# The seventh weight block of a seven-product set: summed ahead into a buffer of its own, or made in place by a difference at its own step

## The chip, the core and the metric

The kernel runs on one core of a Trainium2 chip. The metric is the time of one execution in device microseconds (us); a time quoted for a kernel is the median of several executions. One of the executions was recorded by the hardware profiler, and every row of a profile in this document comes from such a recording.

The engines go by the names of the profile: PE (TensorE) multiplies matrices, and PEld is its loading of weights; DVE (VectorE), ACT (ScalarE) and POOL (GpSimd) work on elements; SP issues transfers. POOL and SP each feed DMA queues of their own.

## What is computed

One block of a language model over 512 tokens of 1024 features, in float32:

```python
x = x + 0.5 * swiglu(rmsnorm(x, g1), w_gu1, w_down1)
x = x + hybrid_mixer(rmsnorm(x, gm), ...)
x = x + 0.5 * swiglu(rmsnorm(x, g2), w_gu2, w_down2)
return rmsnorm(x, final_g)

def swiglu(x, w_gu, w_down):             # 1024 -> 2 x 2816 -> 1024
    g, u = jnp.split(x @ w_gu, 2, axis=-1)
    return (jax.nn.silu(g) * u) @ w_down

def hybrid_mixer(h, ...):
    cb, cc, cu, q, k, v, g_lr, r, ga, gb = split(h @ w_in)
    y_conv = (cb * causal_short_conv(cc * cu, conv_w)) @ w_out_conv
    o = gla_chunked(q, k, v, log_a)      # gated linear attention, 64-token chunks, 4 heads
    y_gla = (rmsnorm_per_head(o) * silu(r)) @ w_out_gla
    return (sigmoid(ga) * y_conv + sigmoid(gb) * y_gla) @ w_o
```

## The kernel before

**Products.** Nearly all of the work is products with weights. Each weight block of 512 KB (128 partitions by 1024 numbers) is loaded into a tile `f`, and is split into two parts that TensorE multiplies faster: ACT casts it to a high part `wh` (line 409), and DVE subtracts that from the block to get the low part `wl` (line 411). PE multiplies `wh` with the high and the low part of the activations, and then `wl` with the high part. A step of the plan is one weight block with its matmuls: in the rows of the profile 16 matmuls of `wh` and 8 of `wl` (line 575), or 8 of `wh` and 8 of `wl` in a wider form (line 587).

**Sets of seven.** The large products are made in sets. A set covers a 2 x 2 grid of weight blocks a11, a12, a21, a22 and does seven products instead of eight, on sums of blocks. Its steps are called m1, p2, q6, p5, q7, p4 and p3. They need as weights, in this order: a11; a12; then a11+a21+a22 (q6); a21+a22 (p5); **a11+a21 (q7)**; a22 (p4); and for p3 the sum of all that is in a12 by then. A set is named below by the number of its first block in the plan: sets 9 to 41 are the up product of the first FFN, 77 and 81 the values of the attention, 85 to 129 the other columns of `w_in` in the mixer, 141 to 153 its output products, 165 to 197 the up product of the second FFN. The steps of neighbouring sets are interleaved: for a set s and its successor t the order is

```python
seq += [(s, "q6"), (s, "p5"), (s, "q7")]
...
    seq += [(t, "m1"), (s, "p4")]
    seq += [(t, "p2"), (s, "p3")] if i + 2 < n else [(s, "p3")]
```

**The sums of blocks.** Three are made in place by DMAs that add (POOL issues them at line 377, and they show as `f<-f`): a21 += a22 three steps ahead of the set's m1; a11 += a21 right behind the cast and the subtraction of m1; a12 += a11 right behind those of p2. The last one *reads* a11; it is called the add of p2 below. The weights of q7 are the one sum that is made by DVE (line 389): s3 = a11 + a21 at the same place as the first add and ahead of it in the program, since it needs a21 as it was loaded. s3 has a tile of its own. The twelve sets of the two down products ("lean" ones) do it otherwise: they subtract a22 from a11 in place at q7 (line 404).

**Buffers.** There are 10 tiles for raw blocks (`SLOTS`). `slot` gives a new block the tile whose last use, by the plan's step numbers, is earliest. So a set takes five of the ten: four that SP loads (line 350) and s3. `wh` and `wl` have three buffers each.

**What sets the order.** `Weights.take` issues casts and subtractions two steps ahead of the products (`Weights(2)`). The order of the instructions on each engine is then set by a scheduler, from the order in which the program was written and its own estimates; each engine runs its instructions in that order and waits at each until what it needs is there. On DVE, between the subtractions of line 411, stand the other uses of the results: line 657 is the sum that takes a product's value out of its PSUM bank (`quarter`), lines 635 and 642 are sums of two halves of a wide bank (`bb`), and lines 561, 1611 and 1625 are elementwise products and sums of the mixer. In the mixer, p5 of a set uses the PSUM bank that p2 of the same set had, so p5's first matmul needs that set's line 657 to be done. On ACT, lines 633 and 634 copy a wide bank, and line 1590 applies an activation.

Of the kernel before, what the change touches and what calls it, by code (L numbers as in the profile page):

```python
# [56 lines left out]
def unit_cols(u):  # L57
    return u[2] * len(u[3]) * u[4]
# [72 lines left out]
def pieces(half):  # L131
    return [min(2, half - k) for k in range(0, half, 2)]
# [16 lines left out]
def lean(n):  # L149
    return PLAN[n][0].endswith("down")  # L150
# [39 lines left out]
def block_kernel(ctx: ExitStack, tc: tile.TileContext, xT, vecs, gf, gup, wgl, wts, out):  # L190
# [19 lines left out]
    def tile_of(pool, shape, dtype=F32):  # L210
        cnt[0] += 1
        return pools[pool].tile(shape, dtype, tag=pool, name=f"{pool}{cnt[0]}")
# [82 lines left out]
    class Weights:  # L295
# [63 lines left out]
        def load_set(self, n):  # L359

            a = {p: STEPS.index((n, p)) for p in SEQ}
            for i in range(self.issued, a["m1"]):
                if STEPS[i][1] is None and STEPS[i][0] not in self.raw:
                    self.raw[STEPS[i][0]] = self.dma(STEPS[i][0], i)
            a21 = self.dma(n + 2, max(a["p5"], a["m1"] + 3))
            a11 = self.dma(n, a["q7"] if lean(n) else a["p2"] + 3)
            if lean(n):
                self.raw[n] = [a11, None, a21, None, a11]
                return
            a22 = self.dma(n + 3, a["p4"])  # L370
            s3 = self.slot(a["q7"])
            a12 = self.dma(n + 1, a["p3"])
            self.raw[n] = [a11, a12, a21, a22, s3]

# [5 lines left out]
        def issue(self):  # L380
            at = self.issued
            self.fetch(at)
            for n in self.loads.get(at, ()):
                self.load_set(n)
            for n in self.sums.get(at, ()):
                a11, a12, a21, a22, s3 = self.raw[n]
                w = unit_cols(PLAN[n])
                if not lean(n):
                    nc.vector.tensor_tensor(out=s3, in0=a11, in1=a21, op=ALU.add)
                self.first[n] = (self.add(a21[:, :w], self.block(n + 3), self.added) if lean(n)  # L390
                                 else self.add(a21, a22))
            for n, i in self.more.get(at, ()):
                a = STEPS.index((n, ("p3", "p4")[i // 2]))
                self.raw[n][i] = self.dma(n + i, a)
            n, p = STEPS[at]
            w = unit_cols(PLAN[n])
            if p is None:
                raw = self.raw[n]
            else:
                a11, a12, a21, a22, s3 = self.raw[n]  # L400
                raw = {"m1": a11, "p2": a12, "q6": a11, "p5": a21, "q7": s3, "p4": a22,
                       "p3": a12}[p]
            if p == "q7" and lean(n):
                nc.vector.tensor_tensor(out=a11[:, :w], in0=a11[:, :w], in1=a22[:, :w],
                                        op=ALU.subtract)
            late = at >= len(STEPS) - len(pieces(HALVES[-1]))
            h = tile_of("op" if late else "wh", [P, 1024], F32R)
            l = tile_of("op" if late else "wl", [P, 1024], F32R)
            self.cast = nc.scalar.copy(h[:, :w], raw[:, :w]).ins  # L409
            with ExitStack() if self.lead is None else tc.issue_after(self.lead):  # L410
                nc.vector.tensor_tensor(out=l[:, :w], in0=raw[:, :w],  # L411
                                        in1=h[:, :w].bitcast(F32), op=ALU.subtract)
            self.lead = None
            if p == "m1":
                twin = n + 4 if STEPS[at + 1] == (n + 4, "m1") else n
                self.add(a11[:, :w], a21[:, :w], self.first[twin])
            if p == "p2":
                self.add(a12[:, :w], a11[:, :w])
            self.issued += 1
            self.ready.append((h, l))  # L420
# [1446 lines left out]
```

## Time and profile before

| | us |
|---|---|
| median of 3 runs | 1142.9 (1142.2 to 1143.33) |
| the profiled execution | 1147.98 |
| its span in the trace | 1146.3 |
| PE busy | 1134.4 (99%) |
| DVE busy | 1001.4 (87%) |
| ACT busy | 713.2 (62%) |
| POOL busy | 135.4 (12%) |
| mean granted clock of PE | 0.998 |

The profiled execution is 1.7 us longer than its span, and 5.1 us longer than the median of the others. A row of the timeline gives the start in us from the start of the span, the duration in us, the engine, the line, the operation, what it writes and reads, how many instructions were drawn together (x8), and in square brackets how long the engine had been idle before it and what ended that. A row of groups gives the same without a start, with the total busy time and the mean in ns, and behind it the idle time before these instructions. A row of waits gives who waited, for whom, the total in us, how many times, and the longest.

### The profile page before, as it was taken

To read this page: it belongs to the slowest core of one execution; us is meant where nothing else is said; L and a number is where in the kernel's file an instruction comes from. 1 tells how busy PE (TensorE), PEld (TensorE's weight loads), DVE (VectorE), ACT (ScalarE), POOL (GpSimd) and SP (SyncE) were. 2 spreads that over 40 slices of the span, in tenths; PEclk is the share of its full clock that TensorE was granted. 3 is DMA by queue.
4 is the path that set the end of the run, shared out by engine and by line. 5 is a ranking of instruction groups with operands and counts; after the bars stand their busy time and mean duration, and the time that the engine had idled before them with its cause. 6 is when DMAs were issued, how large, how long until landed. Compare 5 with 4: busy or idle time off the path is not lost.

```text
span 1146.3 us, 17367 instructions
## 1 busy us (share of the span) xinstructions
PE 1134.4 (99%) x6574; PEld 1002.6 (87%) x6574; DVE 1001.4 (87%) x1247; ACT 713.2 (62%) x967; POOL 135.4 (12%) x178
## 2 busy tenths in 40 slices
PE   9999999999999999999999999999999999999997
PEld 7888888988888889999999988999888888898886
DVE  7998888889888977979799889699899888889987
ACT  8576666667455656666666567555747665666645
POOL 1111111111110111100101100110001101112100
PEclk9999999999999999999999999999999999999999
DMA  9477777869574588876869756577537888977941
GB/s 348 100 195 187 200 176 192 193 146 289 141 258 130 118 195 237 201 188 171 231 159 245 184 162 208 132 172 189 151 92 202 199 228 220 226 184 181 267 105 73
DMA packets 74403, 214.28 MB, mean 187 GB/s; under 512 B 8176, under 2 KB 20592, under 8 KB 74320
## 3 DMA queue, kind: packets, MB, share of 16 engines
q0 software_dynamic: 21376, 76.03, 35.8%
q1 hardware_dynamic: 48304, 132.67, 34.7%
q10 hardware_dynamic: 4640, 4.49, 1.2%
q8 instruction: 51, 0.84, 0.3%
q14 instruction: 32, 0.26, 0.1%
HBM read 133.46 MB, written 11.53 MB: 126 GB/s over the span
## 4 chain that ended last, share of the span: by engine, by line
PE 98%; ACT 1%; DMA 0%; DVE 0%; issue 0%; SPq 0%; ACTq 0%
PE mm L892 16%; PE mm L575 15%; PE bb L587 12%; PE mm L468 9%; PE w L587 9%; PE z L587 8%; PE y L587 7%; PE aux L892 6%; PE mm L482 5%; PE x L587 4%; PE y L575 2%; PE z L575 1%; PE aux L575 1%; PE aux L1501 1%; PE x L575 1%; DMA f<-wts 0%
## 5 line engine op out<-in xcount | busy, mean ns | idle before, releaser
L409 ACT CAST wh<-f 128x1024 fp32r<-128x1024 f32 (+1 forms) x366 | 375.1, 1033 | 284.9 <-PE mm L575 40.7
L411 DVE TENSOR_TENSOR wl<-f,wh 128x1024 fp32r<-128x1024 f32 (+1 forms) x366 | 434.4, 1196 | 52.3 <-ACT wh L409 50.3
L377 POOL DMA_DIRECT2D f<-f x132 | 114.0, 866 | 896.6 <-DVE wl L411 591.0
L892 PE MATMUL mm<-wh,op 128*128 128x512 f32 x536 | 133.7, 389 | 0.0
L575 PE MATMUL mm<-op,wh 128*128 128x256 f32 x960 | 125.7, 284 | 0.0
L575 PEld LDWEIGHTS mm<-op,wh 128*128 128x128 f32 x960 | 119.8, 192 | 0.4
L892 PEld LDWEIGHTS mm<-wh,op 128*128 128x128 f32 x536 | 100.4, 188 | 20.7
L587 PE MATMUL bb<-op,wh 128*128 128x512 f32 x384 | 98.7, 399 | 2.6 <-ACT tp L634 2.3
L587 PEld LDWEIGHTS bb<-op,wh 128*128 128x128 f32 x384 | 69.9, 191 | 15.8 <-ACT tp L634 2.5
L468 PE MATMUL mm<-op,wh 128*128 128x512 f32 x320 | 75.8, 389 | 0.0
L892 PE MATMUL mm<-wl,op 128*128 128x512 f32 x268 | 72.8, 389 | 0.0
L587 PE MATMUL w<-op,wh 128*128 128x512 f32 x288 | 71.8, 391 | 0.1
L468 PEld LDWEIGHTS mm<-op,wh 128*128 128x128 f32 x320 | 60.0, 188 | 12.5
L575 PE MATMUL mm<-op,wl 128*128 128x256 f32 x480 | 67.5, 283 | 0.0
L587 PE MATMUL z<-op,wh 128*128 128x512 f32 x256 | 63.8, 391 | 0.0
L575 PEld LDWEIGHTS mm<-op,wl 128*128 128x128 f32 x480 | 61.9, 192 | 0.1
L587 PEld LDWEIGHTS w<-op,wh 128*128 128x128 f32 x288 | 52.7, 188 | 10.3 <-ACT tp L765 0.3
L892 PEld LDWEIGHTS mm<-wl,op 128*128 128x128 f32 x268 | 50.3, 188 | 10.4
L587 PEld LDWEIGHTS bb<-op,wl 128*128 128x128 f32 x384 | 52.8, 192 | 3.9
L587 PE MATMUL y<-op,wh 128*128 128x512 f32 x224 | 55.9, 391 | 0.0
L587 PEld LDWEIGHTS z<-op,wh 128*128 128x128 f32 x256 | 46.8, 188 | 8.9
L587 PE MATMUL bb<-op,wl 128*128 128x256 f32 x384 | 53.8, 283 | 0.0
(321 smaller groups left out, 1914.4 us busy)
## 6 DMA issues: line engine op xcount, KB each, us to landing
f<-wts SPq DMA_DIRECT2D x215, 512.0 KB, 4.6
f<-f POOLq DMA_DIRECT2D x128, 512.0 KB, 5.2
f<-wts POOLq DMA_DIRECT2D x10, 512.0 KB, 8.8
turn<-tp SPq DMA_DIRECT2D x12, 256.0 KB, 3.6
f<-wts SPq DMA_DIRECT2D x10, 256.0 KB, 4.6
X<-xT SPq DMA_DIRECT2D x8, 256.0 KB, 6.1
xs<-X POOLq DMA_DIRECT2D x8, 256.0 KB, 5.2
tp<-ga SPq DMA_DIRECT2D x8, 256.0 KB, 5.5
```

The costliest lines, as they stand in the source:

```text
L377: self.added = nc.gpsimd.dma_start(out_, a, accum_op=ALU.add).ins
L409: self.cast = nc.scalar.copy(h[:, :w], raw[:, :w]).ins
L411: nc.vector.tensor_tensor(out=l[:, :w], in0=raw[:, :w], in1=h[:, :w].bitcast(F32), op=ALU.subtract)
L468: nc.tensor.matmul(o, w[:, i * P : (i + 1) * P], a[k], start=j == k == 0, stop=j == 2 and k == kt - 1)
L482: nc.tensor.matmul(o[c], w[:, s : s + P], a[k], start=k == 0 and j == 0, stop=k == kt - 1 and j == 2)
L575: nc.tensor.matmul(o[:, e * HW : (e + 1) * HW], w[:, k * HW + e * P : k * HW + (e + 1) * P], a(k), start=self.fresh and j == k == e == 0, ...
L587: nc.tensor.matmul(o[:, e, :n], w[:, k * HW + e * P : k * HW + (e + 1) * P], a(k), start=self.fresh and i == k == 0, stop=i == 1 and k == ...
L892: nc.tensor.matmul(o[t], a(k)[:, t * P : (t + 1) * P], ww[:, i * 512 : (i + 1) * 512], start=fresh and j == k == 0, stop=j == 2 and k == s ...
L1501: nc.tensor.matmul(o[:, b], v[t][:, vc : vc + P], sc[:, b], start=True, stop=t == 0)
```

## The change

For every set whose q7 stands more than two steps behind its p2, the sum s3 and its tile are dropped. a11's tile is kept until q7, and at q7's own step DVE subtracts a22 from it in place, as the lean sets do: a11 is by then a11+a21+a22, so the result is a11+a21. Six sets keep the sum (41, 77, 81, 129, 145 and 197); the 12 lean ones stay as they were; 30 change: eight in each FFN, eleven in the mixer (85 to 125) and 141, 149 and 153.

```diff
             a21 = self.dma(n + 2, max(a["p5"], a["m1"] + 3))
-            a11 = self.dma(n, a["q7"] if lean(n) else a["p2"] + 3)
+            same = lean(n) or a["q7"] - a["p2"] > 2
+            a11 = self.dma(n, a["q7"] if same else max(a["q7"], a["p2"] + 3))
             if lean(n):
                 self.raw[n] = [a11, None, a21, None, a11]
                 return
             a22 = self.dma(n + 3, a["p4"])
-            s3 = self.slot(a["q7"])
+            s3 = a11 if same else self.slot(a["q7"])
             a12 = self.dma(n + 1, a["p3"])
             self.raw[n] = [a11, a12, a21, a22, s3]
@@ in issue(), three steps ahead of m1
-                if not lean(n):
+                if s3 is not a11:
                     nc.vector.tensor_tensor(out=s3, in0=a11, in1=a21, op=ALU.add)
@@ in issue(), at the step itself
-            if p == "q7" and lean(n):
+            if p == "q7" and s3 is a11:
                 nc.vector.tensor_tensor(out=a11[:, :w], in0=a11[:, :w], in1=a22[:, :w],
                                         op=ALU.subtract)
```

In the changed kernel the lines behind the first edit stand one further down: the sum is line 390, the subtraction in place 405, the cast 410, the low part 412, and lines 561, 635, 642, 657, 1611 and 1625 are 562, 636, 643, 658, 1612 and 1626.

Two places in the order of DVE show what moves. The rows are those of the program, each with its line, operation, output, inputs and shape; the number behind a tile's name only tells tiles apart. The first is set 113, in the mixer, from q6 to q7. Before, where `f_5294` is this set's s3, `f_5290` its a11, `f_5288` its a21, and the row at the top makes s3 of the next set, 117:

```order
L389 TENSOR_TENSOR f_5537<-f_5533,f_5531 128x1024
L1611 SCALAR_TENSOR_TENSOR y_3208<-tp_5618,tp_5345 128x2x256
L411 TENSOR_TENSOR wl_5626<-f_5290,wh_5625 128x1024
L657 TENSOR_TENSOR tp_5595<-mm_5622,tp_5595 128x512
L411 TENSOR_TENSOR wl_5655<-f_5288,wh_5654 128x1024
L657 TENSOR_TENSOR tp_5480<-mm_5493,tp_5480 128x512
L561 TENSOR_TENSOR qk_3210<-g_598_3489,qk_3210 128x512
L561 TENSOR_TENSOR y_3208<-acc_5560,tp_5480 128x2x256
L561 TENSOR_TENSOR g_598_3489<-g_597_3488,qk_3210 128x256
L561 TENSOR_TENSOR g_598_3489<-qk_3210,sm 128x256
L561 TENSOR_TENSOR g_597_3488<-g_597_3488,qk_3210 128x4x64
L411 TENSOR_TENSOR wl_5689<-f_5294,wh_5688 128x1024
```

The same stretch of DVE after, from p5 on, where `f_5274` is a11 and `f_5276` a22:

```order
L412 TENSOR_TENSOR wl_5636<-f_5272,wh_5635 128x1024
L658 TENSOR_TENSOR tp_5463<-mm_5476,tp_5463 128x512
L562 TENSOR_TENSOR qk_3202<-g_590_3481,qk_3202 128x512
L562 TENSOR_TENSOR y_3200<-acc_5542,tp_5463 128x2x256
L562 TENSOR_TENSOR g_590_3481<-g_589_3480,qk_3202 128x256
L562 TENSOR_TENSOR g_590_3481<-qk_3202,sm 128x256
L562 TENSOR_TENSOR g_589_3480<-g_589_3480,qk_3202 128x4x64
L405 TENSOR_TENSOR f_5274<-f_5274,f_5276 128x1024
L636 TENSOR_TENSOR tp_5690<-tp_5690,tp_5691 128x512
L562 TENSOR_TENSOR qk_3202<-g_588_3479,qk_3202 128x512
L562 TENSOR_TENSOR g_589_3480<-g_590_3481,sm 128x4x64
L412 TENSOR_TENSOR wl_5671<-f_5274,wh_5670 128x1024
```

The sum of the next set is gone from its place ahead of q6, and this set's subtraction stands behind the three `g` products, with three small instructions between it and the low part of q7.

The second place is set 121, from q6 to q7. Before, `f_5758` is a11 and `f_5762` s3, and `tp_6073<-mm_6100` takes p2's value out of the bank that p5 needs:

```order
L642 TENSOR_TENSOR tp_6073<-bb_6051,tp_6073 128x512
L642 TENSOR_TENSOR tp_6096<-bb_5806,tp_6096 128x512
L411 TENSOR_TENSOR wl_6104<-f_5758,wh_6103 128x1024
L1625 SCALAR_TENSOR_TENSOR y_3208<-tp_6096,y_3208 128x2x256
L657 TENSOR_TENSOR tp_6073<-mm_6100,tp_6073 128x512
L411 TENSOR_TENSOR wl_6134<-f_5756,wh_6133 128x1024
L1625 SCALAR_TENSOR_TENSOR y_3208<-tp_6073,y_3208 128x2x256
L553 RECIPROCAL st_so<-st_so 128x64
L657 TENSOR_TENSOR tp_5967<-mm_5972,tp_5967 128x512
L411 TENSOR_TENSOR wl_6164<-f_5762,wh_6163 128x1024
```

After, with `f_5740` for a11 and `f_5742` for a22:

```order
L643 TENSOR_TENSOR tp_6053<-bb_6031,tp_6053 128x512
L412 TENSOR_TENSOR wl_6083<-f_5740,wh_6082 128x1024
L643 TENSOR_TENSOR tp_6076<-bb_5787,tp_6076 128x512
L405 TENSOR_TENSOR f_5740<-f_5740,f_5742 128x1024
L1626 SCALAR_TENSOR_TENSOR y_3200<-tp_6076,y_3200 128x2x256
L658 TENSOR_TENSOR tp_6053<-mm_6080,tp_6053 128x512
L412 TENSOR_TENSOR wl_6113<-f_5738,wh_6112 128x1024
L1626 SCALAR_TENSOR_TENSOR y_3200<-tp_6053,y_3200 128x2x256
L658 TENSOR_TENSOR tp_5948<-mm_5953,tp_5948 128x512
L412 TENSOR_TENSOR wl_6144<-f_5740,wh_6143 128x1024
```

The subtraction stands right behind q6, so ahead of the row of line 658 that frees p5's bank and ahead of p5's low part. Set 125 has the same order. The order of PE's products, the banks and the buffers of `wh` and `wl` are the same in both kernels.

## The prediction, on record before the changed kernel ran

> **What bounds the kernel.** I read the page first: busy time, and the chain that ended last.
>
> ```profile
> PE 1134.4 (99%) x6574; PEld 1002.6 (87%) x6574; DVE 1001.4 (87%) x1247; ACT 713.2 (62%) x967; POOL 135.4 (12%) x178
> PE 98%; ACT 1%; DMA 0%; DVE 0%; issue 0%; SPq 0%; ACTq 0%
> ```
>
> PE is busy for 1134.4 of 1146.3 us, and 98% of the chain runs over it. A change of the weights' making can therefore hardly help; it can only hurt, by making PE wait. What it could win at most is what PE waits now, so the waits of PE came next, the last two once each and short, then the matmuls at the one place that counts, and eight like them from before it:
>
> ```profile
> PE bb L587 <- ACT tp L634: 2.3, 1, 2.3
> ...
> PE mm L482 <- ACT wh L409: 0.7, 1, 0.7
> PE bb L587 <- DVE tp L642: 0.3, 1, 0.3
> 659.06 2.00 PE L587 MATMUL bb<-op,wh 128*128 128x512 f32 x8
> 676.21 3.40 PE L587 MATMUL bb<-op,wh 128*128 128x512 f32 x8 [2.25 <-ACT tp L634]
> 679.41 1.43 PE L587 MATMUL bb<-op,wl 128*128 128x256 f32 x8
> ```
>
> One stall of 2.25 us, and behind it the same eight matmuls take 3.40 instead of 2.00 us. So a stall of that length costs again in speed: 1.40 here, and 1.43 against 1.12 for the eight that follow (1.12 is the usual time, in a row below), 1.7 in all. The windows say where there is little room, each row with the busy time of PE, PEld, DVE, ACT and POOL, the granted clock, the DMA share and GB/s:
>
> ```profile
> 52.00:227.00 175.00, 175.00 (x1060) 156.87 (x1060) 152.03 (x174) 113.30 (x153) 23.39 (x27) 1.00 0.78 189
> 560.00:660.00 100.00, 100.00 (x699) 93.27 (x698) 92.44 (x127) 63.55 (x86) 11.23 (x13) 1.00 0.76 197
> 660.00:690.00 30.00, 27.41 (x177) 24.98 (x176) 24.87 (x30) 20.80 (x29) 0.86 (x1) 0.94 0.60 163
> ```
>
> In the first FFN (52 to 227 us) PE never idles and DVE has 13% left (152.03 of 175). In the mixer (560 to 660) PE still never idles, but DVE has only 7.6 of 100 us left. The stall shows in the third row, at a clock of 0.94.
>
> **The change: what it removes and adds.** Groups by line and form, and waits:
>
> ```profile
> L389 DVE TENSOR_TENSOR f<-f,f 128x1024 f32<-128x1024 f32 x36 | 44.0, 1221 | 4.1 <-DMA f<-wts 3.5
> L404 DVE TENSOR_TENSOR f<-f,f 128x1024 f32<-128x1024 f32 x10 | 12.2, 1223 | 5.7 <-DMA f<-f 5.7
> L411 DVE TENSOR_TENSOR wl<-f,wh 128x1024 fp32r<-128x1024 f32 x350 | 423.9, 1220 | 51.1 <-ACT wh L409 49.1 <-PE mm L1166 0.9 <-issue 0.3
> POOL f L377 <- DVE f L389: 112.5, 25, 24.2
> ACT wh L409 <- DVE f L404: 25.0, 11, 3.5
> DVE f L404 <- DMA f<-f: 6.0, 7, 1.6
> ```
>
> *DVE's work.* 30 sums of 1.221 us go and 30 differences of 1.223 us come: +0.06 us over the kernel, nothing. What changes is when.
>
> *Loads and the first add.* A set takes four tiles of ten instead of five, so SP's loads can start earlier; and a21 += a22 no longer stands behind the sum (POOL waited 112.5 us for it, 25 times). POOL is 12% busy and none of PE's waits above is for a transfer, so I cost both at nothing; the loads' lead hides them before as after. On POOL's and SP's queues nothing new is issued.
>
> *The new wait.* The difference overwrites a11, so it must wait until the add of p2 (a12 += a11) has landed; DVE stands at it meanwhile, with everything that is behind it in its order. And ACT's cast for q7 now waits for the difference: before, s3 lay ready long ahead. The rows of line 404 show both waits in the lean sets: DVE stood 6.0 us in seven cases, ACT 25.0 in eleven, and PE nothing. So the price is set by the cover at each place, which I went through set by set: landing of the add of p2, plus 1.22 for the difference, plus 1.05 for the cast, against the start of q7's matmuls; and what stands behind the difference on DVE, against the matmul that needs it.
>
> *FFN sets (16).* Set 13, from the add of p2 through q6's low part and q7's cast to q7's matmuls, and the transfer times of that stretch:
>
> ```profile
> 67.93 0.86 POOL L377 DMA_DIRECT2D f<-f  x1 [4.70 <-DVE tp L766]
> 73.07 1.23 DVE L411 TENSOR_TENSOR wl<-f,wh 128x1024 fp32r<-128x1024 f32 x1
> 75.06 1.05 ACT L409 CAST wh<-f 128x1024 fp32r<-128x1024 f32 x1 [1.20 <-PE y L587]
> 81.40 0.86 PE L587 MATMUL z<-op,wh 128*128 128x512 f32 x3
> f<-f POOLq DMA_DIRECT2D x24, 512.0 KB, 5.0
> ```
>
> The add is issued at 67.93 and by the median of 5.0 lands at 72.9, before DVE is done with q6 (74.30). The difference then runs to 75.5, the cast to 76.6, and PE wants it at 81.40: 4.8 us of cover, with DVE pushed back by 1.2 in a stretch where it has 13% to spare. The others look like it: 0. If a landing ran some 5 us late here, PE would begin to wait.
>
> *Place A, set 113 (mixer, 590 us).* Here DVE is the cover that fails.
>
> ```profile
> 582.77 1.22 DVE L389 TENSOR_TENSOR f<-f,f 128x1024 f32<-128x1024 f32 x1
> 586.24 1.22 DVE L411 TENSOR_TENSOR wl<-f,wh 128x1024 fp32r<-128x1024 f32 x1
> 589.85 0.42 DVE L561 TENSOR_TENSOR g<-g,qk 128x256 f32<-128x256 f32 x1
> 590.18 1.22 DVE L411 TENSOR_TENSOR wl<-f,wh 128x1024 fp32r<-128x1024 f32 x1
> 590.18 2.00 PE L587 MATMUL bb<-op,wh 128*128 128x512 f32 x8
> 592.02 1.12 PE L587 MATMUL bb<-op,wl 128*128 128x256 f32 x8
> ```
>
> Before, q7's low part (590.18 to 591.40) follows the third `g` product, 0.6 us ahead of its matmul at 592.02, and the high part was cast long ago. After, the difference stands behind that `g` product, and the cast behind the difference. The sum of 1.22 ahead (582.77) is gone, and DVE comes earlier by up to that; I take 1.1, since a sum of line 657 between them can't come before its matmuls end: difference 589.1 to 590.3, cast to 591.35, matmul at 591.4 instead of 590.18. The low part follows behind three small products, at 591.8 to 593.0, and is wanted at 591.4 + 1.84 = 593.2, in time. **+1.2.** Lower end 0 (DVE gains more from the sums that are gone earlier), upper end 2.3 (it gains nothing, and the difference starts when the `g` product ended, 590.27).
>
> *Places B and C, sets 121 and 125.* Here the landing decides. Adds issued over 560 to 690 us, then that of B alone, and the least, middle and longest landing of the two issued at C:
>
> ```profile
> f<-f POOLq DMA_DIRECT2D x14, 512.0 KB, 6.6
> f<-f POOLq DMA_DIRECT2D x1, 512.0 KB, 8.3
> DMA to landing us min/median/max: 4.7/6.5/8.4
> 625.40 0.86 POOL L377 DMA_DIRECT2D f<-f  x1 [3.35 <-DMA f<-f]
> 627.06 1.22 DVE L411 TENSOR_TENSOR wl<-f,wh 128x1024 fp32r<-128x1024 f32 x1
> 628.19 0.69 DVE L1625 SCALAR_TENSOR_TENSOR y<-tp,y 128x512 f32<-128x512 f32 x1
> 628.79 0.68 DVE L657 TENSOR_TENSOR tp<-mm,tp 128x512 f32<-128x512 f32 x1
> 633.57 1.60 PE L575 MATMUL mm<-op,wh 128*128 128x256 f32 x12
> ```
>
> ```profile
> 645.97 1.21 POOL L377 DMA_DIRECT2D f<-f  x1
> 648.31 1.22 DVE L411 TENSOR_TENSOR wl<-f,wh 128x1024 fp32r<-128x1024 f32 x1
> 650.77 0.68 DVE L657 TENSOR_TENSOR tp<-mm,tp 128x512 f32<-128x512 f32 x1
> 653.38 2.08 PE L575 MATMUL mm<-op,wh 128*128 128x256 f32 x16
> ```
>
> In both sets the difference stands right behind q6's low part, and behind it wait line 1625 (0.69) and the sum of line 657 (0.68) that frees p5's bank. So p5 starts no sooner than landing + 1.22 + 0.69 + 0.68 = landing + 2.6. B: issue 625.40; DVE arrives at 629.0 (q6's low part from 627.06 for 1.22, then one sum of line 643, a row like that of 657, 0.68). With the 8.3 of the trace the add lands at 633.7 and p5 starts at 636.3 instead of 633.57: +2.7. With the median 6.6 it lands at 632.0: +1.0. With 5.0, as in the FFN, 630.4: 0. C: the add of p2 is the second of the two, issued at 645.97; DVE arrives at 650.2 in the same way. With 8.4: 654.4 + 2.6 = 657.0 against 653.38, +3.6. With 6.6: +1.8. With 5.0: +0.2. I take the median of this stretch at both, since the changed kernel's earlier loads and adds will not meet these two at the same moment; the ends are 0.2 and 6.3 for the two together.
>
> The Trainium skill bears on this number (DMA: Bandwidth & Descriptors, Anatomy of one DMA): it fits a DMA on POOL's software path as 2.0 us plus the bytes at 436 GB/s, by which 512 KB would take some 3.2 us, an estimate of mine from its formula. By it B and C would cost nothing, and the sum be 1.2; the trace has nothing so short on this line (4.7 was the least at C), so the rows decide.
>
> *The other mixer and last sets* (85 to 109, 117, 141 to 153): the same reckoning leaves room at each, 85 the least with 1.4 to 2.1 us: 0.
>
> **The sum.** Against the profiled execution 1.2 + 1.0 + 1.8 = +4.0. PE never idles between these places, so nothing is given back later. The profiled execution stands 5.1 us above the median (1147.98 against 1142.9); I add the difference to the median: 1142.9 + 4.0 = **1146.9 us**. The clock's part stays out: three stalls of 1 to 2 us are each shorter than the one that cost 1.7 more.
>
> On that the Trainium skill (TensorE: Matmul & The Clock Gate, What's actually happening) says that the clock halves after an idle window of about 3.4 us. The trace shows slow matmuls after 2.25 us already; by the page no stall of my sum costs speed, and by the row the longer ones may.
>
> **Rivals.** *Hidden.* The landings at B and C come near 5 us and A is covered, as PE never waited for the lean sets: between 1142.9 and some 1144.5 (1.2 of A, 0.2 of C). For it speak the zero of line 404 on PE; against it, that the cover at the three places is counted and short.
>
> *Worse.* The landings are as in the trace: 1.2 + 2.7 + 3.6 = 7.5, and the two longer stalls bring 1.7 each in speed: 1150.4 to 1153.8. For it speak the only rows that show these very adds. Against it: earlier loads spread SP's transfers, which at B run beside the add.
>
> *Faster.* The stall of 2.25 at 674 us goes, with its 1.7 of slow matmuls: 1142.9 - 3.9 = 1139.0. It would take ACT's copies of lines 633 and 634 to come 2.25 us earlier. They follow a cast and two activations there; one of the sums of line 389 before it gives DVE 1.22 back, so this decides only if at least two sums' worth reaches that point and A to C cost nothing. The instructions around it stand in the same order in both kernels, so I give it little.
>
> *That nothing changes* because the differences don't move anything is excluded: 30 of them stand in the new order.
>
> **How the numbers follow.** Less than 0.2%, 2.3 us, a measurement of this kernel can't tell from no change. My forecast (+2.3 to +5.5, landings near the median) has 0.36, *worse* 0.22, *hidden* 0.35, *faster* 0.07. So slower 0.58, same 0.35, faster 0.07. The range leaves out *faster* and the top of *worse*: from 1142.0 (hidden, with a run's spread of about 1 us below) to 1151.5; the forecast's own is 1145.2 to 1148.5.
>
> **What would show it.** In the changed profile: waits of DVE for `f<-f` at line 405, small in the FFNs; waits of PE at line 575 for the sums of line 658 near 634 and 655 us; a wait of PE at line 587 for ACT's cast near 590, of about 1.2; granted clock below 1.00 in 560 to 660. No such PE wait, or landings near 5 us at 625 and 646, would prove the sum wrong; a PE wait in an FFN would mean that landings run later than I counted; and the wait for line 634 near 675 gone would be the third rival.

## The result, and the profile after

The changed kernel takes **1192.9 us** (median of 5 runs, 1191.85 to 1195.22) against 1143.1 for the kernel before: a ratio of 1.0435, with a 95% interval of 1.0417 to 1.0452. That is slower by 50 us, where the prediction said 4 and gave a range that ended at 1151.5.

Busy time, and the chain that ended last, from the page of the changed kernel:

```profile
PE 1149.3 (96%) x6574; PEld 1010.4 (85%) x6574; DVE 998.6 (84%) x1247; ACT 710.3 (60%) x967; POOL 135.4 (11%) x178
PE 12%; DVE 4%; issue 3%; DMA 3%; ACT 1%; ACTq 0%; POOLq 0%
```

The number of PE's instructions is the same, but PE idles 41.9 of 1191.2 us (11.9 of 1146.3 before), and its busy time itself grew by 14.9 us, in good part because matmuls behind some of the stalls run slower (last section). The chain of this page is followed back only to 917 us (its shares add up to 23%); in that stretch it runs over adds in flight, DVE and ACT as well as PE. What PE waits for, longest first (the one at the start and five of at most 1.0 us are left out):

```profile
PE z L588 <- ACT tp L766: 10.8, 5, 2.7
PE w L588 <- ACT tp L766: 6.1, 3, 2.7
PE y L588 <- ACT tp L766: 4.4, 3, 2.7
PE bb L588 <- ACT tp L635: 3.5, 3, 1.8
PE z L588 <- DVE wl L412: 2.9, 3, 1.2
PE y L576 <- ACT tp L762: 2.3, 2, 1.4
...
PE bb L588 <- ACT wh L410: 1.0, 1, 1.0
```

Some three fifths of it is one kind of wait that the prediction never priced: for ACT's copy of a wide PSUM bank in the FFNs (line 766). The windows of the same stretches of work, now later in the execution (first FFN; mixer; the place of the old stall), in the columns of the windows shown before:

```profile
52.00:248.00 196.00, 181.95 (x1056) 159.56 (x1055) 150.50 (x172) 112.72 (x152) 23.42 (x27) 0.97 0.66 159
587.00:687.00 100.00, 98.27 (x680) 90.97 (x679) 93.03 (x128) 60.61 (x83) 10.43 (x13) 1.00 0.71 183
687.00:717.00 30.00, 28.57 (x194) 26.35 (x193) 27.11 (x32) 23.21 (x31) 1.99 (x3) 1.00 0.64 175
```

The first FFN, where PE never idled and where I had put 0, now idles 14 of 196 us. By the starts of PE's steps in the two traces the changed kernel is 20.8 us behind at the end of the first FFN, loses about 19 more in the second, and some 5 in all between. That is the 44.9 us between the two spans; the medians lie 50 apart because the recording of the kernel before was 5.1 us longer than its median.

### The profile page after: what moved, and what is told of

Same layout as the page of the kernel before. It is cut to its first block, busy times and chain, and to the rows that moved or that the text cites. A ratio compares the mean times of both kernels' runs of the same rounds, so it can differ in the third digit from the quotient of the medians.

```text
span 1191.2 us, 17364 instructions
## 1 busy us (share of the span) xinstructions
PE 1149.3 (96%) x6574; PEld 1010.4 (85%) x6574; DVE 998.6 (84%) x1247; ACT 710.3 (60%) x967; POOL 135.4 (11%) x178
## 5 line engine op out<-in xcount | busy, mean ns | idle before, releaser
L405 DVE TENSOR_TENSOR f<-f,f 128x1024 f32<-128x1024 f32 (+1 forms) x42 | 50.3, 1197 | 58.5 <-issue 50.5
L588 PE MATMUL z<-op,wh 128*128 128x512 f32 x256 | 67.6, 408 | 7.7 <-ACT tp L766 7.7
```

What stands on the lines that cost most here:

```text
L588: nc.tensor.matmul(o[:, e, :n], w[:, k * HW + e * P : k * HW + (e + 1) * P], a(k), start=self.fresh and i == k == 0, stop=i == 1 and k == ...
```

## Where the time goes: one set

The waits of the other engines, and the group of the difference, in the changed kernel:

```profile
POOL f L378 <- DMA f<-wts: 297.1, 31, 19.9
ACT wh L410 <- DVE f L405: 68.0, 28, 5.1
DVE f L405 <- issue: 50.5, 16, 4.9
L405 DVE TENSOR_TENSOR f<-f,f 128x1024 f32<-128x1024 f32 x40 | 48.9, 1223 | 58.2 <-issue 50.5 <-DMA f<-f 5.5 <-DVE tp L783 1.4
```

DVE stands 58 us at the differences. "issue" only says that the profile shows no releaser; the difference starts 0.08 us after the add of p2 has landed in each of the sets 13 to 37. And POOL stands 297 us for loads; before it was this:

```profile
POOL f L377 <- DMA f<-wts: 48.1, 4, 18.6
```

Set 17 shows both. POOL's adds before: the second add of set 17 (80.50), the first of set 21 (85.50), the add of p2 of set 17 (86.64).

```profile
80.50 0.86 POOL L377 DMA_DIRECT2D f<-f  x1 [6.78 <-DVE wl L411]
85.50 0.86 POOL L377 DMA_DIRECT2D f<-f  x1 [4.14 <-DMA f<-f]
86.64 0.86 POOL L377 DMA_DIRECT2D f<-f  x1 [0.27 <-DVE wl L411]
```

After, the first add of set 21 stands *ahead* of the second of set 17 in POOL's order. It needs no sum of DVE any more, so the scheduler puts it early; but it needs set 21's block. The three rows of the program on POOL, where `f_869` is set 21's a22, `f_681` set 17's a11 and `f_685` its a12:

```
L378 DMA f_865<-f_869 128x1024
L378 DMA f_681<-f_679 128x1024
L378 DMA f_685<-f_681 128x1024
```

POOL stands 13.72 us for that load, then issues the first two, and later the add of p2:

```profile
84.44 1.75 POOL L378 DMA_DIRECT2D f<-f  x2 [13.72 <-DMA f<-wts]
93.55 0.86 POOL L378 DMA_DIRECT2D f<-f  x1 [7.36 <-DVE tp L775]
```

The two that go out together take 5.3 and 8.1 us from issue to landing, where the second add of set 17 took 5.0 before (first line: the one issued at 80.50 before; second line: the two at 84.44 after):

```profile
DMA to landing us min/median/max: 5.0/5.0/5.0
DMA to landing us min/median/max: 5.3/6.7/8.1
```

The second add, issued at 84.97, so lands at 93.03, and the add of p2, which reads the tile that it writes, follows 0.52 us later; the DVE sum that its row names had ended at 92.65. In twelve of the fourteen FFN sets from 13 to 37 and 169 to 193 the second add went out at most 3.6 us behind the next set's first add, and took 6.4 to 9.6 us to land. In the other two (37 and 193) it went out by itself and took 4.8 and 5.1; before, with 7.6 us or more between it and the add ahead of it, it took 4.5 to 5.5 in all fourteen. Its issue moved less: against m1 by 1.0 us in the median.

The add of p2, issued at 93.55, lands at 100.66. What stands behind it, on DVE, ACT and PE:

```profile
100.74 1.23 DVE L405 TENSOR_TENSOR f<-f,f 128x1024 f32<-128x1024 f32 x1 [3.88 <-issue]
102.48 0.69 DVE L783 TENSOR_TENSOR tp<-x,tp 128x512 f32<-128x512 f32 x1
103.08 1.22 DVE L412 TENSOR_TENSOR wl<-f,wh 128x1024 fp32r<-128x1024 f32 x1
103.20 0.63 ACT L1030 ACTIVATE tp<-tp 128x512 f32<-128x512 f32 x1 [4.87 <-DVE tp L783]
103.74 1.98 ACT L410 CAST wh<-f 128x1024 fp32r<-128x1024 f32 x2
104.45 1.19 PE L588 MATMUL z<-op,wl 128*128 128x256 f32 x8 [1.21 <-DVE wl L412]
105.95 0.69 DVE L775 TENSOR_TENSOR tp<-w,tp 128x512 f32<-128x512 f32 x1
106.67 0.63 ACT L1045 ACTIVATE tp<-tp 128x512 f32<-128x512 f32 x1 [0.95 <-DVE tp L775]
107.67 0.59 ACT L766 COPY tp<-y 128x512 f32<-128x512 f32 x1
108.31 2.12 PE L588 MATMUL y<-op,wh 128*128 128x512 f32 x8 [0.84 <-ACT tp L766]
```

DVE stands 3.88 us. Behind the difference on DVE is a sum of line 783; for that sum ACT's activation of line 1030 waits 4.87 us; behind it in ACT's order stand q7's cast, the next set's cast, an activation of line 1045 (which waits 0.95 us more, for a sum of line 775 that is late on DVE too), and at last the copies that free q6's bank, into which q7 accumulates. So q7 starts 7.65 us after the landing. It does so in nine of the fourteen sets; in four (25, 33, 181 and 189) it starts 4.9 to 5.2 us after it, and at set 185 the add lands in time. PE starts q7 16.7 us behind the set's m1 when nothing stops it, so the add of p2 had to land within 9.1 us of m1 in the nine, and within 11.5 in the four. In the trace *before*, it landed 7.5 to 11.1 us behind m1 in the fourteen sets; after, 8.5 to 14.1. At set 13, where the prediction saw a cover of 4.8 us, this chain leaves 0.8 (a landing 8.3 us behind m1); at sets 17, 173, 177 and 193 it leaves none.

## The experiments

Each time is set against the kernel before, run beside it (1142.5 to 1143.3 us).

| kernel | what it changes | us | ratio (95%) |
|---|---|---|---|
| the change | | 1192.9 | 1.0435 (1.0417 to 1.0452) |
| e_five | five tiles a set | 1192.6 | 1.0434 (1.0419 to 1.0450) |
| e_pool | POOL's order as before | 1173.6 | 1.0264 (1.0247 to 1.0281) |
| e_own | no wait for the add of p2 | 1163.9 | 1.0178 (1.0156 to 1.0201) |
| e_late | difference later on DVE | 1155.2 | 1.0108 (1.0093 to 1.0123) |
| e_both | e_late and e_pool | 1155.2 | 1.0105 (1.0090 to 1.0120) |
| e_ownlate | e_own and e_late | 1147.8 | 1.0041 (1.0026 to 1.0056) |
| e_all | e_own, e_late and e_pool | 1145.1 | 1.0017 (1.0009 to 1.0026) |
| e_none | no difference at all | 1142.4 | 0.9994 (0.9984 to 1.0003) |
| e_ffn | the change in the FFNs alone | 1186.5 | 1.0388 (1.0364 to 1.0412) |
| e_mix | the change outside the FFNs alone | 1153.6 | 1.0095 (1.0080 to 1.0110) |
| e_abc | sets 113, 121 and 125 alone | 1151.5 | 1.0077 (1.0063 to 1.0091) |
| e_abcpool | e_abc, POOL's order as before | 1148.6 | 1.0038 (1.0025 to 1.0051) |

**POOL's order.** `e_pool`:

```diff
-                                 else self.add(a21, a22))
+                                 else self.add(a21, a22, self.behind))
...
-                self.add(a11[:, :w], a21[:, :w], self.first[twin])
+                self.behind = self.add(a11[:, :w], a21[:, :w], self.first[twin])
```

> The changed kernel with one edit: the first add of a set (a21 += a22) may not be issued by POOL ahead of the second add of the set before it (a11 += a21), which is the order of the kernel before. Theory queue (the loss is that POOL, in order, stands at the next set's first add until its block is loaded, and so issues this set's second and third add late, 5 to 8 us): most of the loss goes, 1145 to 1152 us. Theory place (the loss is where the difference stands on DVE, ahead of p5's low part; the adds would land late anyhow): little changes, 1180 to 1193. Theory loop (late difference, late low part of p5, late load into the tile that it frees, late first add, late second and third add of the next set, late difference again; any link that is cut ends it): 1145 to 1152. Theory tiles (four tiles a set bring the loads at worse times): 1185 to 1193.

It gave 1173.6: 19 of the 50 us go. None of the four theories said that. The wait for loads is nearly gone, but DVE stands at the differences almost as long:

```profile
POOL f L379 <- DMA f<-wts: 65.4, 6, 20.3
DVE f L406 <- issue: 45.8, 17, 4.3
```

So POOL's order is a part of the loss, not all of it. With it, the second adds of the fourteen FFN sets land in 4.6 to 6.2 us again.

**The place on DVE.** `e_late`, where `self.low` is the instruction of the last low part:

```diff
             if p == "q7" and s3 is a11:
-                nc.vector.tensor_tensor(out=a11[:, :w], in0=a11[:, :w], in1=a22[:, :w],
+                with ExitStack() if lean(n) else tc.issue_after(self.low):
+                    nc.vector.tensor_tensor(out=a11[:, :w], in0=a11[:, :w], in1=a22[:, :w],
...
```

> The changed kernel with one edit: on DVE the difference of a changed set stands behind the low part of p5 (line 412) instead of ahead of it. POOL's order stays that of the changed kernel. Theory queue: the adds are as late as before, so most of the loss stays, 1175 to 1193 us. Theory place: most goes, 1145 to 1152. Theory loop: p5's low part frees its tile in time, the loads and so the adds come early again, 1145 to 1155. Theory tiles: 1185 to 1193.

1155.2, just above what the theories place and loop had: with the instructions the same and the difference of each changed set moved by a few places, 38 of the 50 us go. POOL still stands for loads, and the adds still land late (10.0 to 13.6 us behind m1 in the FFN sets), but DVE now does the sum that was line 783 and p5's low part before it comes to the difference (line 406 here), and hardly waits:

```profile
POOL f L378 <- DMA f<-wts: 237.5, 27, 20.2
DVE f L406 <- DMA f<-f: 12.3, 13, 1.6
DVE f L406 <- issue: 5.8, 4, 2.1
```

That speaks for place, and against my theory loop: the low part of p5 was early again, and POOL's waits for loads stayed. They do not come from the late difference.

**Tiles.** `e_five` gives each set its fifth tile again, unused:

```diff
-            s3 = a11 if same else self.slot(a["q7"])
+            s3 = self.slot(a["q7"])
+            if same:
+                s3 = a11
```

> The changed kernel, but a fifth tile is given to each set and left unused; the difference is in place, and waits for the add of p2. Theory tiles: the loads come as before the change and the loss goes, 1143 to 1155 us. Theories queue, place and loop: the wait and the orders are those of the changed kernel, so 1180 to 1205.

1192.6: the number of tiles is not the cause.

**No wait for the add of p2.** `e_own` writes the difference into that fifth tile:

```diff
-            s3 = a11 if same else self.slot(a["q7"])
+            s3 = self.slot(a["q7"])
...
-                nc.vector.tensor_tensor(out=a11[:, :w], in0=a11[:, :w], in1=a22[:, :w],
+                nc.vector.tensor_tensor(out=s3[:, :w], in0=a11[:, :w], in1=a22[:, :w],
...
```

> The changed kernel, but the difference is written into a tile of its own (five tiles a set, as before the change), so it needs only a11 with a21 added and a22, and does not wait for the add of p2. POOL issues as in the changed kernel, the difference is made at q7's step. All theories but tiles say that the wait for the add of p2 is the start of the loss: 1143 to 1150 us. Theory tiles expects the same, since five tiles are back; the next kernel parts them.

1163.9, a miss of all theories. In the first FFN nothing is lost; in the second 10.5 us are, and 8 at sets 141 to 153. The scheduler put these differences earlier, right where the *second* add (a11 += a21) should have landed, and DVE stood there:

```profile
DVE f L406 <- DMA f<-f: 67.2, 28, 6.5
```

Free of one transfer, the instruction was placed to wait for another. This too is place.

**Edits together.** `e_both` is `e_late` with `e_pool`; `e_ownlate` is `e_own` with `e_late`; `e_all` is all three.

> The changed kernel with both edits, POOL's order of the first and second adds as before the change and the difference behind p5's low part on DVE. Theory loop (difference ahead of p5's low part, and POOL's order, feed each other; place is the stronger link, since its edit alone left 1155 us and POOL's alone 1174): 1140 to 1148, the rest of e_late goes. Theory place alone (POOL's order has no part of its own): like e_late, 1153 to 1157.

1155.2, the same as `e_late`: with the difference in the later place, POOL's order has no part of its own that shows.

> e_own (the difference into a fifth tile, no wait for the add of p2) with the difference behind p5's low part on DVE. In e_own DVE stood 67 us at differences that were placed too early, for the add that completes a11. Theory place: with this edit DVE comes to the difference when a11 is ready, PE waits nowhere for it: 1138 to 1146 us. Theory wait (the add of p2 is what matters and the place does not): like e_own, 1160 to 1166.

1147.8: 7.5 us less than `e_late`, so that much goes with the wait for the add of p2 where the place is mended. It is still 5.0 us above the kernel before.

> e_ownlate with POOL's order of the kernel before as well: no wait for the add of p2, the difference behind p5's low part, the first add of a set behind the second of the set before. e_ownlate alone stands 5.0 us above the kernel before. If late adds of a11 are what is left there: 1142 to 1145 us. If it is the 1.22 us of DVE and the cast behind it at q7's time, and not the adds: like e_ownlate, 1146 to 1149.

1145.1, at the edge of the first expectation. POOL's order, and so by the expectation the late second adds, made up 2.7 of these 5.0 us. Of the rest, 2.4 us (1.0009 to 1.0026), its trace shows 1.2 at the prediction's place A: q7 of set 113 starts 1.2 us later, behind the difference and the cast.

```profile
591.18 2.12 PE L591 MATMUL bb<-op,wh 128*128 128x512 f32 x8 [1.05 <-ACT wh L413]
```

What is left of it was not parted further.

**No difference.** `e_none` leaves the 30 differences out, with loads, tiles and adds as in the changed kernel; what q7 multiplies by is then not what the reference needs:

```diff
-            if p == "q7" and s3 is a11:
+            if p == "q7" and lean(n):
```

> The changed kernel without the 30 differences: q7 of these sets multiplies by a11 with all its sums in it, so the output is not the reference's. Loads, tiles and adds stay. Theory place and loop: no instruction of DVE waits for the add of p2, so the loop is open: 1135 to 1147. Theory queue in its strong form (POOL's order delays a11 and so q6 itself): 1160 or more.

1142.4, the time of the kernel before. POOL stands for loads as in the changed kernel, and nothing is lost by it:

```profile
POOL f L378 <- DMA f<-wts: 231.4, 27, 20.5
673.21 2.00 PE L588 MATMUL bb<-op,wh 128*128 128x512 f32 x8
```

So late adds cost only where an instruction with something behind it waits for them. The second row is the place of the stall of 2.25 us in the trace before: here there is none, and this profiled execution took 1142.95, 0.5 above its median. The stall and its 1.7 us of slow matmuls are thus most of the 5.1 us by which the recording of the kernel before exceeds its own median; that most executions of that kernel lack it is likely, but not shown. The run also shows that less work on DVE had nothing to win: DVE is busy 968.7 us here, against 1001.4 before, and the time is the same.

**Parts of the plan.** `e_ffn`, `e_mix` and `e_abc`, one line each:

```diff
-            same = lean(n) or a["q7"] - a["p2"] > 2
+            same = lean(n) or a["q7"] - a["p2"] > 2 and PLAN[n][0].endswith("gu")
+            same = lean(n) or a["q7"] - a["p2"] > 2 and not PLAN[n][0].endswith("gu")
+            same = lean(n) or n in (113, 121, 125)
```

> The change in the 16 sets of the two FFNs alone; the mixer's and the last products' sets keep the sum. Theory loop: the FFNs lose what they lost in the changed kernel (20.8 us in the first, some 19 in the second by the steps of PE), and nothing of it is given back, since PE is the bound between: 1180 to 1186 us. The recorded prediction had 0 for these sets: 1143.

1186.5, at the upper edge of the expectation: 43.8 of the 50 us are the FFNs'.

> The change in the mixer and the last products alone (14 sets); the 16 sets of the FFNs keep the sum in a fifth tile. By the changed kernel's trace the loss between set 77 and set 165 was 4.9 us, about 1.2 of it at set 113 and 3.6 at sets 85 to 89, with 2.5 us back at set 129. Theory loop, per stretch: 1144 to 1149. The recorded prediction expected 1146.9 from these sets alone. A rival, that late loads carry over from one stretch to the next and the mixer inherited its loss from the FFN: 1140 to 1143.

1153.6: 10.9 us, more than both expectations. Its trace loses 3.0 us at sets 85 and 89, 1.2 at place A, 0.5 at B and 1.0 at C, and has a stall of 2.2 us at set 129. The two parts sum to 54.7, 4.7 more than the whole change costs, so they are not independent; why was not settled.

> The change in the three sets 113, 121 and 125 alone, the places A, B and C of the recorded prediction, which had 1.2 + 1.0 + 1.8 = 4.0 us for them: 1146.9. By the changed kernel's trace A costs 1.2, B nothing and C 0.5: 1143.5 to 1145.5.

1151.5: 8.8 us, a miss upward. Place A cost 1.2. At B, PE lost 5.0, and most of the rest is a stall of 1.7 us at set 129. The rows tell of B: the second add of set 121 stood behind the first of set 125 on POOL, and went out 0.5 us behind it.

```profile
619.23 1.75 POOL L378 DMA_DIRECT2D f<-f  x2 [16.68 <-DMA f<-wts]
630.87 0.86 POOL L378 DMA_DIRECT2D f<-f  x1 [9.89 <-issue]
635.49 1.22 DVE L405 TENSOR_TENSOR f<-f,f 128x1024 f32<-128x1024 f32 x1 [2.13 <-issue]
637.23 0.68 DVE L658 TENSOR_TENSOR tp<-mm,tp 128x512 f32<-128x512 f32 x1
638.06 3.44 PE L576 MATMUL mm<-op,wh 128*128 128x256 f32 x16 [3.44 <-DVE tp L658]
```

The add of p2 landed at 635.4, 4.5 us after its issue: the landing was *shorter* than any I had counted with. The issue was at 630.87, though, where I had taken 625.40: it followed the landing of the second add, 10.6 us after that one's issue. The chain behind it is the predicted one: difference, line 1626, line 658, p5.

`e_abcpool` puts the first adds of the sets around these three where they stood on POOL before the change, with `self.behind` as in `e_pool`:

```diff
-                                 else self.add(a21, a22))
+                                 else self.add(a21, a22, self.added if n in (117, 121) else self.behind))
```

> e_abc (the change in sets 113, 121 and 125 alone, 1151.5 us) with POOL's order of the adds around these sets as in the kernel before, which is the order that the recorded sum took for granted. In e_abc PE lost 1.2 us at A and 5.0 at B, where the second add of set 121 stood behind the first of set 125. Theory late adds: B falls to what a landing of 5 to 8 us from 625 gives (0 to 2.7), A stays 1.2: 1143.5 to 1148. If POOL's order has no part in it: like e_abc, 1150 to 1153.

1148.6, a little above the first expectation, and this kernel's runs spread from 1145.9 to 1150.8. Its profiled execution (1146.2, one of the faster) shows A at 1.2, B and C at 0, and a stall of 2.2 us at set 129 like the one in the trace before. So in this execution B fell as expected; where the slower ones lose 2 to 5 us more is open.

## Why the prediction was wrong

- **The first add (step "Loads and the first add", priced at nothing): wrong, and here the error begins.** I wrote that it no longer stands behind the sum, and did not ask ahead of what it would then stand. The instruction that lost a wait was placed earlier in an in-order queue, and handed its other wait to those behind it. POOL was 12% busy and yet stood 297 us. The standing by itself cost nothing (`e_none`); but the first add that ended it went out together with the second add of the set before, whose landing grew from 4.6 to 7.5 us (median of the fourteen FFN sets) and held back the add of p2. Undoing this alone gave back 19 us in the whole change (`e_pool`).
- **FFN sets (0): 43.8 us (`e_ffn`). The step that failed is the cover.** I followed the difference to q7's cast, and p5's low part by a general share of 13% free time on DVE. I did not follow the sum of line 783, which stands behind the difference, to ACT, nor the bank's copies that stand behind it there. By that chain, 7.65 us from landing to q7 in nine of fourteen sets, the adds of the trace before were already at the limit or up to 1.6 us inside it, and lateness beyond that goes straight into PE. Moving the difference behind the sum and the low part gave back 38 us (`e_late`).
- **Landings.** I took 5.0 us for the FFNs and 6.6 for the mixer. The 5.0 is a median over all three kinds of add; the add of p2 by itself took 6.3 in the fourteen FFN sets before, and 5.8 after, so its length was not the trouble. Its issue was: 3.1 us behind m1 before, 6.0 after (medians), for want of the second add, whose landing I had not looked at. On the whole page the median went from 5.2 to 5.8:

```profile
f<-f POOLq DMA_DIRECT2D x128, 512.0 KB, 5.8
```

- **Place A (+1.2): right.** The difference behind the `g` products, the cast behind it, PE 1.05 us idle; the step q7 came 1.2 us later in the changed kernel, in `e_abc` and in `e_abcpool`:

```profile
615.81 1.22 DVE L405 TENSOR_TENSOR f<-f,f 128x1024 f32<-128x1024 f32 x1
617.06 1.99 ACT L410 CAST wh<-f 128x1024 fp32r<-128x1024 f32 x2 [1.09 <-DVE f L405]
618.16 2.12 PE L588 MATMUL bb<-op,wh 128*128 128x512 f32 x8 [1.05 <-ACT wh L410]
```

- **Places B and C (+1.0, +1.8): mechanism right, size by chance.** In the changed kernel B cost nothing and C 0.5; in `e_abc` B cost 5.0; in `e_abcpool` neither cost anything. In `e_abc` what decided was when POOL issued the add (10.7 us behind m1, where it was 6.1 before), which I had held fixed. In the changed kernel B's add was issued 5.8 us behind m1 and landed in 5.9 us instead of 8.3, shorter than the 6.6 that I took.
- **The stall as something to lose: half right.** "Faster" was priced at 3.9 us from a stall that lies in the profiled execution. In the changed kernel some 3 us of it do go, but the medians had nothing to give, as `e_none` shows.
- **The clock's part (left out): wrong.** PE's busy time grew by 14.9 us, with stalls of up to 2.7 us; some 8.5 of it is the clock (last section).
- **The direction was right, in good part by luck:** the three places that it rests on gave 1.7 us in the changed kernel, and the sets that were put at 0 gave the rest. Of the rows named as signs, the wait of DVE at line 405 told ("small in the FFNs", but 58 us, two thirds of it there), and PE's wait near place A came, with 1.05 us; the waits of PE for line 658 and the lower clock in the mixer did not (it was 1.00).

My theory of a loop through the loads fell (`e_late`, `e_none`). What the runs support is a product of two things: an add that lands late, and a place on DVE ahead of work that PE needs. Take away either the difference (`e_none`) or, for the most part, its place (`e_late`), and the lateness of the adds costs little. In `e_pool`, where POOL's order is the old one, the adds of p2 still land 10 to 13 us behind m1: they are issued at 3.9 us (3.1 before) and take 6.9 (6.3 before) in the median of the fourteen sets. What makes landings longer, there and for two adds that go out together, was not settled.

## What to carry to other kernels

When an edit removes a dependency, look at the order of *every* in-order queue on which something could now move up, transfer-issuing queues too, and ask which other wait it brings to the front. When an instruction gets a wait, follow all that stands behind it on its engine, then what stands behind the waiters on the next engine, until PE; the cover is the shortest of these chains, not the one through the data. A result made long ahead is worth its buffer where the engine that makes it is in the path of everything else; if it must be made late, place it behind the work that others wait for.

## What the hardware showed

Matmuls behind a stall of a few us are often slower for a while, but not always. In `e_abc` above, sixteen that take 2.08 us took 3.44 behind 3.44 us of idleness. In the changed kernel eight that take 2.00 took 3.45 behind 2.74 us, at a granted clock of 0.50 (the column ahead of the DMA share), but 2.12 behind 0.84 (row at 108.31 above). And behind another 2.74 us nothing was slow:

```profile
84.65 3.45 PE L588 MATMUL z<-op,wh 128*128 128x512 f32 x8 [2.74 <-ACT tp L766]
85.10:88.50 3.40, 3.40 (x11) 2.75 (x10) 2.76 (x3) 0.76 (x2) 1.09 (x2) 0.50 0.95 220
1049.29 1.22 PE L588 MATMUL z<-op,wl 128*128 128x256 f32 x8 [2.74 <-ACT tp L766]
1050.35 2.00 PE L588 MATMUL z<-op,wh 128*128 128x512 f32 x8
```

Of the changed kernel's seven stalls of 2.2 to 2.8 us, five were followed by 3.41 us at a granted clock of 0.50, which began up to 1.5 us behind the restart; two were not (those that ended at 962.93 and 1049.29). One of 1.75 us was, too. Half the clock for 3.41 us costs about 1.7 us. There are six such stretches, against one in the trace before, so they make up some 8.5 of the 14.9 us by which PE's busy time grew; the rest was not taken apart. So a stall of 2.7 us in this kernel costs 2.7 or about 4.4, and which of the two was not predicted by its length. The granted clock of the whole stretch (0.97 over the first FFN) shows it only as a mean.
